# Down-projection loads of `final_g` and of the residual on other queues; the output projection's weights split during the attention, kept in DRAM, and read back as halves by GpSimd

## The chip, the cores and the metric

The kernel runs on one core of one Trainium2 chip. The metric is the device time of one execution in microseconds; of the kernel before there are three runs. A core has TensorE (PE in the rows, matrix products), VectorE (DVE), ScalarE (ACT), GpSimd (POOL) and SyncE (SP, which here only issues transfers). Each engine works through its own list in order; engines wait for one another by semaphores. Transfers between DRAM and the on-chip memory are issued by an engine (an instruction that ends once the transfer is handed over) and carried by 16 DMA engines that all queues share.

## What is computed

One inference step of a one-layer decoder: 1024 prompt rows and 8 x 4 = 32 sample rows, 1024 features, in float32.

```python
mod = jax.nn.silu(c) @ w_ada + b_ada            # shift, scale, gate, twice
h = _rmsnorm(x, norm1_g) * (1 + sc1) + sh1
mix, new_conv, new_kv = _mixer(h, w_in, conv_w, gn_conv, gn_attn, w_out, rel_bias, conv_prev, kv_bufs)
x = x + ga1 * mix                               # output projection: mixed @ w_out
h2 = _rmsnorm(x, norm2_g) * (1 + sc2) + sh2
ffn = (jax.nn.silu(h2 @ w_gate) * (h2 @ w_up)) @ w_down
x = x + ga2 * ffn
y = _rmsnorm(x, final_g)
```

The mixer is one input projection `w_in` into convolution inputs and queries, keys and values; a short convolution; dilated window attention in three groups of four heads (rows of the prompt among themselves, sample rows against caches); a norm; and the output projection `w_out` (1024 x 1024). The caches, moved on by four rows, are outputs too.

## The kernel before

**Numbers.** Every float32 product is made as three products of rounded halves: high x high, low x high, high x low. So each weight tile is loaded (`load_raw`, L117: a tile of 128 x 1024, 512 KB, in one of three slots of the tag `raw`), its high half `wh` is made by ScalarE (`split_high`, through the helper at L93) and its low half `wl` = raw - wh by VectorE (`split_raw`, L136). The tags `wh` and `wl` have two slots each; a slot is free once the last reader of the tile in it is done. Activations have halves as well (`mh`/`ml`, `xh`/`xl`, `ah`/`al`).

**Stages,** in order of time: to 67 us the first norm and the conditioning; 67 to 484 us the input projection, tile by tile of 128 columns (`proj_res`, three products of column blocks of 384, 384 and 288 rows each), woven with the prompt attention of six pairs (group g, pair j) and the sample attention. In the loop over g and j, a pair's three tiles (key, query, value) are multiplied, then `prompt_pair` runs; products of the pair after are woven into it. 484 to about 608 us is the output projection: `w_out_tile(m)` (L1182) loads and splits tile m with SP, ScalarE and VectorE; tiles 0 to 7 are multiplied with column blocks 0 and 1 of the mixer's output, and once more, loaded and split again, with blocks 2 and 3 (16 tiles in all). Meanwhile `mixed` (L1106 on) makes the halves `mh` and `ml` of the next block, `squares` and `norm2_square` add up sums of squares, and the second norm (`modulate`, L265 to L276) and `combos(0)` (L1215 on: sums of column blocks and their halves `xh`, `xl`, for a fast matrix product with seven multiplications) prepare the FFN. 608 to 1081 us is gate and up of the FFN; GpSimd makes the sums of weights that the fast product needs (L1325 to L1328) and stores each finished block of silu(gate) x up to `a_d` in DRAM (L1420). From 1105 us the down projection runs in four chunks: `load_a` (L1468) loads the six pieces `a` of a chunk from `a_d`, on SP, into slots of the tag `raw`, and ScalarE and VectorE make `ah` and `al`; `load_down` loads `w_down` tiles into the same three slots; the residual `x2m` is read from `xT_d` (8 pieces of 528 KB).

**What sets the order.** Each engine's list is in the order in which the scheduler of the language places the instructions; `high_priority` moves a load or a split ahead as far as its slots allow, `in_order` and `issue_after` place one behind another. Engine and queue are written in the code: `nc.gpsimd.tensor_sub` is GpSimd's arithmetic, `nc.sync.dma_start` a transfer issued by SP. The copies of the caches (L1412) are issued by SP, two after each FFN step, the remaining ones behind the last weights. In `mixed`, GpSimd makes three of four `ml` (`k % 4`); in `squares` and `norm2_square` the argument `eng` names the engine that adds.

## Time and profile before

| | us |
|---|---|
| median of 3 runs | 1382.58 (1374.85 to 1383.36) |
| profiled execution, its own time | 1384.71 |
| its span in the profile | 1382.9 |
| TensorE busy | 1304.9 (94%) |
| VectorE busy | 722.4 (52%) |
| ScalarE busy | 505.1 (37%) |
| GpSimd busy | 252.5 (18%) |
| bytes moved | 199.81 MB, mean 144 GB/s |

The page and the views of the trace count an engine as busy while an instruction of it runs (issuing a transfer, waiting and semaphores are not counted). A row's "idle before" is the time in which the engine stood still just before that instruction, and the name behind the arrow is what ended it. The granted clock (PEclk) is TensorE's clock as a share of its upper level of 2.4 GHz; the lower level is 1.2 GHz, or 0.50. Times in the rows are in us from the span's start; L12 is line 12 of the kernel before.

### The profile page before, as it was taken

Reading aid. Unit: us, or ns where it says so; the run is one execution under the profiler, and the core shown is the slowest. Engines: PE = TensorE matmul, PEld = TensorE weight load, DVE = VectorE, ACT = ScalarE, POOL = GpSimd, SP = SyncE. Lnnn points to the kernel's source line nnn. Section 1 sums busy time; section 2 is a strip of 40 time slices with the busy share of each in tenths; the row PEclk is TensorE's granted clock in tenths of the full one; section 3 lists DMA queues with packets and bytes.
Section 4 is the critical chain, followed back from the end, with each engine's and each line's share of the span. In section 5 each row is a group of like instructions: output and inputs, shape, how many; then the busy total and the mean of one; then the engine's idle time right before and its main releaser. Section 6 shows DMA issues by size and latency. Waiting matters only on the chain.

```text
span 1382.9 us, 23582 instructions
## 1 busy us (share of the span) xinstructions
PE 1304.9 (94%) x9488; PEld 1207.1 (87%) x9488; DVE 722.4 (52%) x1399; ACT 505.1 (37%) x1085; POOL 252.5 (18%) x251
## 2 busy tenths in 40 slices
PE   8999999998999989897999999999999399999996
PEld 7777686887779879887999999999999299999996
DVE  5722364155227767889654466455445335353466
ACT  5432414243342255646334334333334202020244
POOL 3700000000000146354222334223212100000000
PEclk9999999998989999999999999999999799999998
DMA  9975371247336624464352634333250824141344
GB/s 313 302 243 166 103 264 48 67 126 225 99 102 173 178 71 154 139 218 136 110 192 84 227 93 168 123 108 110 90 205 32 307 58 140 46 140 47 94 145 133
DMA packets 189500, 199.81 MB, mean 144 GB/s; under 512 B 11786, under 2 KB 166919, under 8 KB 188880
## 3 DMA queue, kind: packets, MB, share of 16 engines
q1 hardware_dynamic: 176718, 173.76, 39.7%
q0 software_dynamic: 5600, 20.59, 4.1%
q10 hardware_dynamic: 7074, 3.97, 1.1%
q8 instruction: 74, 1.21, 0.4%
q14 instruction: 34, 0.28, 0.1%
HBM read 169.53 MB, written 55.82 MB: 163 GB/s over the span
## 4 chain that ended last, share of the span: by engine, by line
PE 76%; DVE 8%; DMA 8%; ACT 3%; issue 3%; POOL 1%; SPq 1%; DVEq 0%; ACTq 0%; POOLq 0%
PE pss L1381 6%; PE pss L1382 6%; PE pss L1383 6%; PE psmm L161 5%; PE psmm L162 4%; PE psmm L163 4%; PE pss L1494 3%; PE pss L1495 3%; PE pss L1496 3%; PE psmm L1494 3%; PE psmm L1495 3%; PE psmm L1496 3%; DMA qb<-qs_d 3%; PE pss L683 3%; PE psmm L1381 3%; PE psmm L1382 3%
## 5 line engine op out<-in xcount | busy, mean ns | idle before, releaser
L93 ACT ACTIVATE wh<-raw 128x512 fp32r<-128x512 f32 (+2 forms) x208 | 160.9, 785 | 423.1 <-PE psmm L162 96.7
L1381 PE MATMUL pss<-xh,wh 128*128 128x264 f32 x704 | 201.3, 286 | 5.2 <-DVE sg L1358 2.3
L1383 PE MATMUL pss<-xh,wl 128*128 128x264 f32 x704 | 201.2, 286 | 2.6 <-DVE wl L1318 2.5
L1382 PE MATMUL pss<-xl,wh 128*128 128x264 f32 x704 | 201.1, 286 | 1.8 <-DVE xl L1227 1.8
L161 PE MATMUL psmm<-hh,wh 128*128 128x384 f32 (+1 forms) x528 | 176.8, 335 | 2.3 <-DVE ring L1041 1.4
L162 PE MATMUL psmm<-hl,wh 128*128 128x384 f32 (+1 forms) x528 | 175.3, 332 | 0.0
L163 PE MATMUL psmm<-hh,wl 128*128 128x384 f32 (+1 forms) x528 | 174.9, 331 | 0.0
L136 DVE TENSOR_TENSOR wl<-raw,wh 128x1024 fp32r<-128x1024 f32 (+2 forms) x111 | 117.1, 1056 | 78.2 <-ACT wh L93 77.2
L1318 DVE TENSOR_TENSOR wl<-raw,wh 128x512 fp32r<-128x512 f32 x96 | 90.1, 950 | 115.6 <-ACT wh L93 112.5
L1381 PEld LDWEIGHTS pss<-xh,wh 128*128 128x128 f32 x704 | 133.5, 190 | 6.5 <-DVE sg L1358 2.5
L1383 PEld LDWEIGHTS pss<-xh,wl 128*128 128x128 f32 x704 | 132.7, 189 | 3.7 <-DVE wl L1318 3.6
L1382 PEld LDWEIGHTS pss<-xl,wh 128*128 128x128 f32 x704 | 133.4, 189 | 2.1 <-DVE xl L1227 2.1
L161 PEld LDWEIGHTS psmm<-hh,wh 128*128 128x128 f32 x528 | 101.0, 191 | 16.5 <-issue 12.9
L1494 PE MATMUL pss<-ah,wh 128*128 128x384 f32 (+1 forms) x264 | 86.5, 328 | 23.8 <-ACT wh L93 23.8
L163 PEld LDWEIGHTS psmm<-hh,wl 128*128 128x128 f32 x528 | 101.4, 192 | 3.1 <-issue 2.7
L162 PEld LDWEIGHTS psmm<-hl,wh 128*128 128x128 f32 x528 | 100.9, 191 | 3.2 <-issue 2.9
L1381 PE MATMUL psmm<-xh,wh 128*128 128x264 f32 x352 | 101.0, 287 | 1.4 <-ACT p L93 0.8
L1383 PE MATMUL psmm<-xh,wl 128*128 128x264 f32 x352 | 100.8, 286 | 0.4 <-DVE wl L1318 0.4
L1382 PE MATMUL psmm<-xl,wh 128*128 128x264 f32 x352 | 100.9, 287 | 0.0
L1495 PE MATMUL pss<-al,wh 128*128 128x384 f32 (+1 forms) x264 | 86.3, 327 | 0.0
L1496 PE MATMUL pss<-ah,wl 128*128 128x384 f32 (+1 forms) x264 | 86.1, 326 | 0.0
L1495 PE MATMUL psmm<-al,wh 128*128 128x384 f32 (+1 forms) x264 | 85.5, 324 | 0.0
(327 smaller groups left out, 2925.6 us busy)
## 6 DMA issues: line engine op xcount, KB each, us to landing
ring<-in_w_ada_dram SPq DMA_DIRECT2D x32, 512.0 KB
out_dram<-in_cache_kv_dram SPq DMA_DIRECT2D x8, 2040.0 KB
raw<-in_w_in_dram SPq DMA_DIRECT2D x24, 512.0 KB
raw<-in_w_gate_dram SPq DMA_DIRECT2D x24, 512.0 KB
raw<-in_w_up_dram SPq DMA_DIRECT2D x24, 512.0 KB
a_d<-sg POOLq DMA_DIRECT2D x22, 528.0 KB, 3.7
a<-a_d SPq DMA_DIRECT2D x22, 528.0 KB
raw<-in_w_down_dram SPq DMA_DIRECT2D x48, 192.0 KB
```

Source lines behind the costliest of these rows:

```text
L93: return nc.scalar.activation(out, in_, func, **kw)
L136: nc.vector.tensor_sub(wl[:, :nk], raw[:, :nk], wh[:, :nk].bitcast(F32))
L161: nc.tensor.matmul(out, wh[:, k], h, start=(i == 0), stop=False)
L162: nc.tensor.matmul(out, wh[:, k], l, start=False, stop=False)
L163: last = nc.tensor.matmul(out, wl[:, k], h, start=False, stop=(i == n - 1))
L1318: nc.vector.tensor_sub(wl[:, 4 * i:4 * i + 4], x, h.bitcast(F32))
L1381: nc.tensor.matmul(o, wh[:, k0 + k], hi[:, k], start=st, stop=False, skip_group_check=True)
L1382: nc.tensor.matmul(o, wh[:, k0 + k], lo[:, k], start=False, stop=False, skip_group_check=True)
L1383: last = nc.tensor.matmul(o, wl[:, k0 + k], hi[:, k], start=False, stop=(k == 3), skip_group_check=True)
L1494: nc.tensor.matmul(o[:, :n], wh, ah[:, t0:t0 + n], start=(j == 0), stop=False)
L1495: nc.tensor.matmul(o[:, :n], wh, al[:, t0:t0 + n], start=False, stop=False)
L1496: nc.tensor.matmul(o[:, :n], wl, ah[:, t0:t0 + n], start=False, stop=(j == 2 * nf - 1))
```

## The change

1. `fg` (`final_g` to 128 rows) was loaded by ScalarE's queue at the start of the last chunk; now GpSimd's queue loads it after `load_a(0)`. The eight residual pieces `x2m` were loaded by GpSimd's queue; now SP loads each behind the weights of its tile in the first chunk.
2. `split_out(m)` loads tile m of `w_out`, splits it and has GpSimd store both halves in DRAM (`wo_d[m]`): one tile after each pair of the attention, two in group 1. `w_out_tile` no longer loads and splits: GpSimd issues two loads of 512 KB, the high half into a slot of `raw`, the low half in turn into a slot of `wh` or `wl`.
3. The additions that GpSimd did around the output projection (`ml`, sums of squares, `combos(0)`, the sample columns in `modulate`) are VectorE's.

```diff
--- before.py
+++ after.py
@@ -105,6 +105,7 @@
     strip_d = dr.tile([12, NSTRIP], F32, name="strip_d")
     st_d = dr.tile([3, 64, P], F32, name="st_d")
     wgt_d = dr.tile([3, 32, P], F32, name="wgt_d")
+    wo_d = [dr.tile([2, P, D], F32R, name=f"wo_d{m}") for m in range(KT)]
     qs_d = dr.tile([3, NS, 256], F32, name="qs_d")
 
     def rstd_from(ss_ap, n, out_ap):
@@ -272,8 +273,8 @@
         if n_p < n:
             tv = x[:, :, o + n_p:o + n]
             t4 = tv.rearrange("p k (b t) -> p k b t", t=NT)
-            nc.gpsimd.tensor_mul(t4, t4, bcast(amod[:, 1, :, 1:9], 3, NT))
-            nc.gpsimd.tensor_add(t4, t4, bcast(modt[:, 3, :, 1:9], 3, NT))
+            nc.vector.tensor_mul(t4, t4, bcast(amod[:, 1, :, 1:9], 3, NT))
+            nc.vector.tensor_add(t4, t4, bcast(modt[:, 3, :, 1:9], 3, NT))
 
     w_in_v = w_in[0].rearrange("(k p) c -> p k c", p=P)
 
@@ -911,6 +912,14 @@
             else:
                 nc.vector.tensor_scalar(bss[g][:, P:], mask[:, 1], new[:, 0:1], None, op0=ALU.add)
 
+    w_out_v = w_out[0].rearrange("(k p) c -> p k c", p=P)
+
+    def split_out(m):
+
+        for i, x in enumerate(split_raw(load_raw(w_out_v[:, :, P * m:P * m + P], KT), KT)):
+            nc.gpsimd.dma_start(wo_d[m][i].rearrange("p (k c) -> p k c", c=P), x)
+
+    out_split = iter(range(KT))
     bss = [cp.tile([P, 160], F32, name=f"bs{g}") for g in range(3)]
 
     yt = []
@@ -947,6 +956,8 @@
             store_kvp(g, k_n, 0, j, 7 if g == 0 else (1 if g == 1 else 0))
             if j and g == 0:
                 sample_bias()
+            for _ in range(2 if g == 1 else 1):
+                split_out(next(out_split))
         stats_out(g)
         queues["any"].append(sample_scores(g, *sample_new(g, qs, ks, vs)))
         yt += qs
@@ -1093,7 +1104,7 @@
     feats = [(c, 0) for c in conv] + [(y, DIL[i // 2]) for i, y in enumerate(yt)]
     acc_y = squares(feats[2:], 0, nc.vector)
     rb_y = rstd_rows(acc_y, 0, 768, "rbb1", after_gate, "pt")
-    acc_m = squares(feats[2:], 1, nc.gpsimd)
+    acc_m = squares(feats[2:], 1, nc.vector)
     conv_gate(1)
 
     m_hi = [[unit(ua, "mh", (P, 2, NSUB), F32R) for _ in range(4)] for _ in range(2)]
@@ -1115,12 +1126,10 @@
                 nc.vector.scalar_tensor_tensor(dst(t[:, sl]), src(x), sv[:, gcol:gcol + 1], dst(rbb[:, sl]),
                                                op0=ALU.mult, op1=ALU.mult)
             act(hi, t[:, :n])
-            eng = nc.gpsimd if k % 4 else nc.vector
-            eng.tensor_sub(m_cols(m_lo, tb, k), t[:, :n], hi.bitcast(F32))
-
-    w_out_v = w_out[0].rearrange("(k p) c -> p k c", p=P)
+            nc.vector.tensor_sub(m_cols(m_lo, tb, k), t[:, :n], hi.bitcast(F32))
+
     order = list(range(2, KT)) + [0, 1]
-    rot = [0]
+    rot = [0, 0]
 
     def psb():
         rot[0] += 1
@@ -1180,7 +1189,13 @@
         return last
 
     def w_out_tile(m):
-        return load_w(w_out_v[:, :, P * m:P * m + P], KT)
+        hi = wp.tile([P, T], F32R, tag="raw", bufs=3, name=nm("wh"))[:, :D].rearrange("p (k c) -> p k c", c=P)
+        rot[1] += 1
+        lo = wp.tile([P, KT, P], F32R, tag=("wh", "wl")[rot[1] % 2], bufs=2, name=nm("wl"))
+        with tc.high_priority():
+            for i, x in enumerate((hi, lo)):
+                nc.gpsimd.dma_start(x, wo_d[m][i].rearrange("p (k c) -> p k c", c=P))
+        return hi, lo
 
     acc_x = {}
 
@@ -1209,7 +1224,7 @@
         mixed(tb, range(2), rstd_rows(acc[1], tb, 256, "rbb0", after))
 
     def mixed_squares(tb):
-        return squares(feats[2:], tb, nc.gpsimd), squares(feats[:2], tb, nc.gpsimd)
+        return squares(feats[2:], tb, nc.vector), squares(feats[:2], tb, nc.vector)
 
 
 
@@ -1256,9 +1271,9 @@
     for m in range(2, KT):
         w_o = w_out_tile(m)
         out_product(w_o, m, 0)
-        norm2_square(0, m, nc.gpsimd)
+        norm2_square(0, m, nc.vector)
         last = out_product(w_o, m, 1)
-        norm2_square(1, m, nc.gpsimd if m < 6 else nc.vector)
+        norm2_square(1, m, nc.vector)
         if m == 3:
             sample_merge()
             acc_m = mixed_squares(3)
@@ -1278,7 +1293,7 @@
         norm2_square(2, m, nc.vector)
         out_product(w_o, m, 3)
         norm2_square(3, m, nc.vector)
-    combos(0, [ua] * 4 + [ub] * 3, nc.gpsimd)
+    combos(0, [ua] * 4 + [ub] * 3, nc.vector)
     xa.release()
     w3 = tc.alloc_tile_pool(name="w3", bufs=1, reuse_waits="tile")
     w1 = tc.alloc_tile_pool(name="w1", bufs=1, reuse_waits="tile")
@@ -1497,22 +1512,22 @@
         add_gated(5, m, t0, n, x2m[m][:, t0:t0 + n], o)
 
     a = load_a(0)
-    for m in range(KT):
-        x = (d1 if m < 7 else d2).tile([P, T], F32, tag="x2", bufs=7 if m < 7 else 1, name=nm("x2"))
-        nc.gpsimd.dma_start(x, xT_d[:, m])
-        x2m.append(x)
+    fg = d2.tile([P, D], F32, name="fg")
+    nc.gpsimd.dma_start(fg, bcast(final_g, 0, P))
     for c, (f0, nf) in enumerate(CHUNKS):
         if f0 + nf < FH:
             for m in range(KT):
                 w = load_down(f0, nf, m)
+                if c == 0:
+                    x = (d1 if m < 7 else d2).tile([P, T], F32, tag="x2", bufs=7 if m < 7 else 1, name=nm("x2"))
+                    nc.sync.dma_start(x, xT_d[:, m])
+                    x2m.append(x)
                 for t0, n in TBS:
                     down(w, a, nf, m, t0, n)
             a = load_a(c + 1)
             continue
         with in_order(silu[0]):
             nc.scalar.preload_act_table_set("natural_log_exp_and_others")
-        fg = d2.tile([P, D], F32, name="fg")
-        nc.scalar.dma_start(fg, bcast(final_g, 0, P))
         for tb, (t0, n) in enumerate(TBS):
             for m in range(KT):
                 down(load_down(f0, nf, m), a, nf, m, t0, n)
```

How this moves the lists, at three places. First, ScalarE in the attention, at what the trace of before has from 183 to 210 us (`ring` are the emptied products of `w_in` tiles, `wh` the high halves). Before:

```order
L93 ACTIVATE wh_1529<-raw_1527 128x1024
L93 ACTIVATE ring_1396<-psmm_1403 128x384
L93 ACTIVATE ring_1396<-psmm_1448 128x384
L93 ACTIVATE wh_1904<-raw_1902 128x1024
L93 ACTIVATE ring_1396<-psmm_1487 128x256
L93 ACTIVATE ring_1396<-psmm_1487 128x32
L93 ACTIVATE ring_1526<-psmm_1533 128x384
L93 ACTIVATE ring_1526<-psmm_1571 128x384
L93 ACTIVATE wh_2042<-raw_2040 128x1024
```

Now:

```order
L93 ACTIVATE wh_1545<-raw_1543 128x1024
L93 ACTIVATE ring_1412<-psmm_1419 128x384
L93 ACTIVATE ring_1412<-psmm_1464 128x384
L93 ACTIVATE wh_1885<-raw_1883 128x1024
L93 ACTIVATE ring_1412<-psmm_1503 128x256
L93 ACTIVATE ring_1412<-psmm_1503 128x32
L93 ACTIVATE wh_1928<-raw_1926 128x1024
L93 ACTIVATE ring_1542<-psmm_1549 128x384
L93 ACTIVATE ring_1542<-psmm_1587 128x384
L93 ACTIVATE wh_2066<-raw_2064 128x1024
```

One `wh` more (`wh_1885`, from the first `w_out` tile of that stretch) stands between the emptied products, and the next `w_in` tile's `wh_1928` comes later in the list.

Second, SP where the down projection begins (`a` are the pieces of the FFN's result, `x_16..` to `x_17..` the residual, `raw` the `w_down` tiles, `out_dram` the last cache copies). Before:

```order
L1412 DMA out_dram<-in_cache_kv_dram 16x16256 x2
L1412 DMA out_dram<-in_cache_kv_dram 16x3968 x8
L1472 DMA a_11554<-a_d_83 128x1056
L1472 DMA a_11560<-a_d_83 128x1056
L1472 DMA a_11566<-a_d_83 128x1056
L1472 DMA a_11572<-a_d_83 128x1056
L1472 DMA a_11578<-a_d_83 128x1056
L1472 DMA a_11584<-a_d_83 128x1056
L1487 DMA raw_11606<-in_w_down_dram 128x3x128 x2
L1487 DMA raw_11676<-in_w_down_dram 128x3x128 x2
L1487 DMA raw_11746<-in_w_down_dram 128x3x128 x2
```

Now:

```order
L1427 DMA out_dram<-in_cache_kv_dram 16x3968 x8
L1487 DMA a_11594<-a_d_83 128x1056
L1487 DMA a_11600<-a_d_83 128x1056
L1487 DMA a_11606<-a_d_83 128x1056
L1523 DMA x_1687_11639<-xT_d 128x1056
L1487 DMA a_11612<-a_d_83 128x1056
L1487 DMA a_11618<-a_d_83 128x1056
L1487 DMA a_11624<-a_d_83 128x1056
L1523 DMA x_1695_11711<-xT_d 128x1056
L1502 DMA raw_11632<-in_w_down_dram 128x3x128 x2
L1502 DMA raw_11704<-in_w_down_dram 128x3x128 x2
L1523 DMA x_1703_11783<-xT_d 128x1056
```

The residual pieces, which stood in GpSimd's list, are now between the `a` pieces and the `w_down` tiles.

Third, GpSimd in the output projection (`acx` sums of squares, `ml` low halves; `wo_d` the stored halves of `w_out`). Before:

```order
L1197 TENSOR_TENSOR acx_5003<-acx_5003,sq_5424 128x272
L1197 TENSOR_TENSOR acx_5129<-acx_5129,sq_5453 128x256
L1197 TENSOR_TENSOR acx_5003<-acx_5003,sq_5488 128x272
L1197 TENSOR_TENSOR acx_5129<-acx_5129,sq_5517 128x256
L1119 TENSOR_TENSOR ml_4914<-mx_5525,mh_4906 128x256
L1119 TENSOR_TENSOR ml_4914<-mx_5530,mh_4906 128x256
L1119 TENSOR_TENSOR ml_4915<-mx_5540,mh_4907 128x256
L1119 TENSOR_TENSOR ml_4916<-mx_5545,mh_4908 128x256
```

Now, at about the same place:

```order
L1197 DMA wh_5456<-wo_d_94 128x1024
L1197 DMA wl_5519<-wo_d_95 128x1024
L1197 DMA wl_5457<-wo_d_94 128x1024
L1197 DMA wh_5518<-wo_d_95 128x1024
L1197 DMA wl_5629<-wo_d_96 128x1024
L1197 DMA wh_5628<-wo_d_96 128x1024
L1197 DMA wl_5691<-wo_d_97 128x1024
L1197 DMA wh_5690<-wo_d_97 128x1024
```

GpSimd's list there holds loads and no additions; the additions stand in VectorE's list.

## Rows read from the trace of the kernel before

**Rows 1.** The page, busy time of two engines: us, share of the span, instructions

```profile
PE 1304.9 (94%) x9488; PEld 1207.1 (87%) x9488; DVE 722.4 (52%) x1399; ACT 505.1 (37%) x1085; POOL 252.5 (18%) x251
```

**Rows 2.** Table of stretches: engines' busy us (instructions), clock, DMA share, GB/s

```profile
core 0: us, PE busy (x) PEld busy (x) DVE busy (x) ACT busy (x) POOL busy (x), PEclk, DMA share, GB/s
300.00:320.00 20.00, 20.00 (x129) 20.00 (x128) 15.08 (x24) 4.42 (x6) 0.00 (x0) 1.00 0.89 278
320.00:340.00 20.00, 15.78 (x85) 13.06 (x83) 11.79 (x28) 6.73 (x17) 1.05 (x2) 0.80 0.74 224
480.00:680.00 200.00, 179.29 (x1320) 168.43 (x1320) 155.41 (x235) 111.31 (x223) 89.81 (x77) 0.96 0.45 140
580.00:600.00 20.00, 15.28 (x110) 14.62 (x108) 20.00 (x23) 8.98 (x12) 9.10 (x3) 0.91 0.19 55
1090.00:1100.00 10.00, 0.00 (x0) 0.00 (x0) 3.77 (x3) 3.25 (x3) 2.17 (x5) 0.50 1.03 411
```

**Rows 3.** Waits: engine, line, waited for; us in total, times, longest

```profile
PE pss L1494 <- ACT wh L93: 23.8, 1, 23.8
```

**Rows 4.** Waits of SP's queue from 1040 to 1130 us

```profile
SPq L1412 <- DMA fg<-in_final_g_dram: 51.4, 1, 51.4
```

**Rows 5.** Timeline of SP: start us, us, line, operation, count

```profile
1012.91 63.92 SPq L1412 DMA_DIRECT2D out_dram<-in_cache_kv_dram  x10
1077.00 10.64 SPq L1472 DMA_DIRECT2D a<-a_d  x6
```

**Rows 6.** Timeline of ScalarE before the down projection

```profile
1081.11 1.08 ACT L93 ACTIVATE ah<-a 128x1056 fp32r<-128x1056 f32 x1 [7.80 <-DMA a<-a_d]
...
1091.15 1.08 ACT L93 ACTIVATE ah<-a 128x1056 fp32r<-128x1056 f32 x1 [5.14 <-DMA a<-a_d]
...
1104.21 0.84 ACT L93 ACTIVATE wh<-raw 128x768 fp32r<-128x768 f32 x1 [7.72 <-DMA raw<-in_w_down_dram]
```

**Rows 7.** Timeline of VectorE at the same place

```profile
1081.30 0.43 DVE L1355 TENSOR_TENSOR sg<-sg,pss 128x264 f32<-128x264 f32 x1 [1.05 <-PE pss L1383]
1082.22 1.26 DVE L1477 TENSOR_TENSOR al<-a,ah 128x1056 fp32r<-128x1056 f32 x1 [0.49 <-ACT ah L93]
```

**Rows 8.** The tile `a_d`: its stores' ns (min/median/max), and their landing

```profile
L1420 POOL DMA_DIRECT2D a_d<-sg x22: 670/682/827, 652.1 to 1082.0; - x22
...
DMA to landing us min/median/max: 3.1/3.7/9.4
```

**Rows 9.** DMA issues from 1076 to 1104 us: count, KB each, median us to landing

```profile
x<-xT_d POOLq DMA_DIRECT2D x8, 528.0 KB, 9.1
```

**Rows 10.** Groups by line, 480 to 680 us: busy us, mean ns; idle before, releasers

```profile
L163 PE MATMUL pss<-mh,wl 128*128 128x272 f32 (+1 forms) x128 | 39.0, 305 | 4.7 <-DVE wl L136 4.7
...
L136 DVE TENSOR_TENSOR wl<-raw,wh 128x1024 fp32r<-128x1024 f32 x19 | 24.0, 1261 | 6.0 <-ACT wh L93 6.0
...
L1381 PE MATMUL pss<-xh,wh 128*128 128x264 f32 x80 | 23.8, 298 | 4.7 <-DVE sg L1358 2.3 <-ACT xh L93 1.9 <-ACT p L93 0.4
L1382 PE MATMUL pss<-xl,wh 128*128 128x264 f32 x80 | 23.6, 295 | 1.8 <-DVE xl L1227 1.8
...
L1227 DVE TENSOR_TENSOR xl<-x,xh 128x1056 fp32r<-128x1056 f32 x14 | 22.4, 1618 | 0.4 <-ACT xh L93 0.4
...
L1119 DVE TENSOR_TENSOR ml<-mx,mh 128x272 fp32r<-128x272 f32 (+1 forms) x8 | 5.7, 716 | 0.0
```

**Rows 11.** The same stretch by form of operation, VectorE

```profile
L1236 DVE TENSOR_TENSOR x<-x 128x1056 f32<-128x1056 f32 x1 | 2.3, 2341 | 0.0
```

**Rows 12.** Groups by form, 680 to 1080 us, VectorE

```profile
L1355 DVE TENSOR_TENSOR sg<-sg,u 128x264 f32<-128x264 f32 x21 | 9.2, 439 | 0.7
```

**Rows 13.** Waits in 480 to 680 us

```profile
POOL x L1234 <- DVE xl L1227: 17.9, 1, 17.9
```

**Rows 14.** Timeline of ScalarE in the attention

```profile
183.63 1.06 ACT L93 ACTIVATE wh<-raw 128x1024 fp32r<-128x1024 f32 x1 [12.99 <-PE psmm L162]
...
197.42 1.06 ACT L93 ACTIVATE wh<-raw 128x1024 fp32r<-128x1024 f32 x1 [2.95 <-PE psmm L162]
```

## The prediction

> **What bounds the kernel now.** I read the page's busy table first [rows 1]: TensorE works in 94% of the span, VectorE in half of it. So only two things can give time: TensorE's idle time (1382.9 - 1304.9 = 78 us) and stretches in which its granted clock is at the lower level. The table of stretches [rows 2] then says where the two lie. From 300 to 320 us TensorE is never idle, though the DMA engines are 0.89 busy. From 320 to 340 it has a stall, after which the mean granted clock is 0.80. In 480 to 680 us (output projection, second norm, start of the FFN) it is idle for 200.0 - 179.3 = 20.7 us; in 580 to 600, where it loses 4.7 us of these, VectorE is busy without a break (20.00 of 20). From 1090 to 1100 it does nothing at all, while the DMA engines are full (1.03, 411 GB/s). That last hole is the passage from the FFN's gate/up to the down projection; the waits of TensorE [rows 3] make it the longest of all: one wait of 23.8 us, for the high half of the first w_down tile. Elsewhere TensorE runs without gaps, and nothing that the change does there can be gained.
>
> **Part 1: the passage to the down projection (x2 and final_g).** Why is that first half late? Backward through the rows: ScalarE makes it at 1104.21, having waited 7.72 us for the w_down load [rows 6]. That load needs one of three `raw` slots, which the six `a` pieces hold; the first `a` piece comes only at 1081.11, after 7.80 us of waiting [rows 6]. SP issues the `a` loads only from 1077.00 on [rows 5], because the last cache copies ahead of them in its order stood for 51.4 us behind one wait: for the load of final_g [rows 4], which ScalarE issues at the very end of the FFN. Once loose, the six `a` loads, the 8 x2 loads of 528 KB on GpSimd's queue (9.1 us to land, [rows 9]) and the weights share the full DMA engines, so that the fourth `a` (needed to free a slot) is split at 1091.15.
> The change takes final_g out of that chain (GpSimd loads it after its last a_d store), and SP's order puts x2 piece 0 behind three `a`, x2 piece 1 before the first w_down tile, the others behind later weights (order, second place). Now SP reaches the `a` loads in time, and three of them lie in their slots before the last gate/up product. Their high halves can be made at about 1074, but VectorE's low halves stand behind the FFN's last product at 1081.30 + 0.43 [rows 7]: the three follow at 1.26 us each, 1083.0, 1084.3, 1085.5. The fourth `a` is issued at 1083, lands 3.7 us later (the median of a_d stores of the same size, [rows 8]), at 1086.7; with 1.08 + 1.26 it frees its slot at 1089. Then 393 KB of w_down: some 2.5 us by its size against 528 KB in 3.7, and 0.84 of ScalarE: TensorE starts at about 1092.5. The bytes give a second bound: two a_d stores, x2 pieces 0 and 1, three `a`, final_g and w_down 0 are seven times 0.54 plus 0.52 plus 0.39 = 4.7 MB, which at 0.38 MB/us (the level of [rows 2] in this hole, a little under 411) is 12.4 us from 1081.3: 1093.7 + 0.84 = 1094.5. Before, it started at 1104.21 + 0.84 = 1105.1. I take 1094: **-11 us**, between -4 (x2 piece 1 waits for the last a_d store, whose longest landing is 9.4, [rows 8], and w_down stands behind it on SP) and -15 (TensorE at 1090).
>
> **Part 2: the output projection.** 16 weight splits leave this stage: 16 passes of ScalarE, which has room, and 16 x 1.261 = 20.2 us of VectorE [rows 10]. GpSimd issues 32 loads of 512 KB in their place (order, third place); the nearest row are the a_d stores, of that size and on that queue: 0.68 to issue and 3.7 to land, 9.4 at most [rows 8]. A tile's 48 products (8 row blocks, 3 products, 2 column blocks) take TensorE 48 x 179.29/1320 = 6.5 us [rows 2], so 2 x 0.68 of issue and 1 MB per tile fit. The loads run three tiles ahead for high halves, four for low ones. GpSimd's arithmetic moves to VectorE: 24 low halves `ml`, 17 + 10 sums of squares, 4 sums in `combos(0)` and 2 products of the sample rows. Their price on VectorE: with GpSimd at work beside it, `ml` took 0.716 [rows 10] and a sum of 1056 columns 2.34 [rows 11]; without, an add of 264 columns took 0.439 and the al subtraction of 1056 columns 1.26 [rows 7, 11, 12]. So between 53 x 0.44 + 4 x 1.26 = 28 us and 53 x 0.72 + 4 x 2.34 = 48 us. Since GpSimd's arithmetic is gone from most of the stage, I take 30. VectorE is at 155.4 of 200 us now [rows 2]; 155.4 - 20.2 + 30 = 165, and what is left also gets cheaper: the 14 `xl` of 1618 ns [rows 10] would take 1.26 as `al` does, -5 us. So VectorE is no fuller than before, and its work is not in the same places: the `wl` on which TensorE waited 4.7 us [rows 10] are gone, and the 4.7 + 1.8 us that the FFN's first products waited for `sg`, `xh` and `xl` [rows 10] came with a `combos(0)` that ran late: GpSimd's first sum waited 17.9 us for an `xl` [rows 13]. On VectorE it stands right behind that `xl`, during the second pass of the output projection. The trap of a new wait: the `ml`, one per product of the next column block, now stand in VectorE's order beside the residual adds. I take half of the 20.7 us: **-10 us**, between 0 and -18 (nearly all of the idle time, with a few us of slow clock behind the stalls).
> *A rule and the rows.* A sum of 1056 columns takes VectorE 2.34 us beside GpSimd's, a subtraction of that size 1.26 with GpSimd idle [rows 7, 11]; I priced most of the moved work at the lower level, since GpSimd is then idle. The Trainium skill, SBUF — State Buffer, section Who interferes with whom, gives the reason: a VectorE instruction with two SBUF inputs contends with a GpSimd instruction that reads SBUF, and the later one waits. By it the moved work costs 28 us and VectorE comes to 163 of 200; by the dear rows 48 and 183, which is the first rival. The same page's section 🔬 SBUF: two separate sides speaks against the change: a load that GpSimd issues waits for its descriptors while VectorE runs a two-port form, and it gives 3.1 us for 0.62; estimated from that page, two loads would take 6.2 us of GpSimd's time per tile, under the tile's own, so the sum would stay.
>
> **Part 3: the attention pays.** The 8 splits of w_out move into 67 to 484 us: one after each pair, two in the middle group. Each adds a 512 KB read, a ScalarE and a VectorE pass (1.06 and 1.26), and two stores of 512 KB that GpSimd issues. ScalarE and VectorE have room there, so the passes cost nothing themselves; they hide under a w_in tile's products, 13.8 us of TensorE (the `wh` of two tiles start at 183.63 and 197.42, [rows 14]). The catch is the slots: `wh` and `wl` have two each, and one turn of them is now a split's. The order of ScalarE (first place below) shows `wh_1928` behind `wh_1885`; it can be written only when the stores out of that slot have landed. Chain: 1.06 + 1.26 + 0.68 + 3.7, then 1.06 + 1.26 for the next tile = 9.0 us: it fits 13.8. With the longest landing (9.4) it is 14.7, or 0.9 too long. With two splits in a row (2 pairs) it is 6.7 + 6.7 + 2.3 = 15.7, some 2 us too long each, 27 at the longest landing, 13 too long. Added to it is the clock: the stall of some 4 us in 320 to 340 left it at half for a while, and its slice fell to 0.80 [rows 2], 4 us of work lost. So two stalls of 2 us: **+4 us**, between -2 (ring loads earlier, since the bias loads have moved up in SP's order) and +44 (both longest cases everywhere: 4 x 0.9 + 2 x 13 = 30, and clock losses of 14).
>
> **Sum.** 1384.7 (profiled execution) - 11 - 10 + 4 = 1367.7. That execution stands 2.1 us over the median of 1382.58, so the median comes to **1366 us**.
>
> **Rivals.**
> - *VectorE fills up* in 484 to 620: it is the one engine at 20.00 of 20 [rows 2], and the `ml` of one column block, `combos(0)` and the residual adds queue on it. For it: 28 to 48 us added against 20 removed. Against it: the 5 us of relief from `xl`. Then part 2 gives -2: 1382.58 - 11 - 2 + 4 = 1374.
> - *x2 ahead of the weights:* the wait of x2 piece 1 for the last store holds the first w_down on SP; only -5 of part 1: 1372.
> - *The other side: the stores' round trip.* On DMA engines at 0.89 [rows 2] each split's stores land late, and `wh` of the next w_in tile keeps ScalarE, and behind it the emptying of PSUM, waiting. Price +44: 1382.58 - 21 + 44 = 1406. It decides above 35/8, about 4.4 us a split, for slower by 1%; above 2.6 a split for no gain.
> - *Both* of the first two, with splits at 2 us each (+16): 1382.58 - 5 - 2 + 16 = 1392.
> - *The change does not do what it says:* the copies still stand behind something on SP: final_g's wait is gone from the order, so the chance is small, within the second rival.
>
> **How the numbers follow.** About 1% is what a measurement of this kernel can tell from no change: 1368.8 and 1396.4 are the bounds. Forecast 0.5 (own range 1356 to 1374, of it 0.4 under 1368.8); VectorE full 0.17; x2 ahead 0.13; round trip 0.1; both 0.1. Faster: 0.4 + 0.05 + 0.05 = 0.50. Slower: 0.1 + 0.02 = 0.12. Same: 0.38. The range leaves out the round trip (0.1) and the worse half of both (0.05) above 1392, and 0.05 below 1353 (the best ends of all parts together give 1382.58 - 15 - 18 - 2 = 1348).
>
> **What would show it.** Right: in the new trace the idle time before the first w_down product is 13 us, not 23.8, SP shows no wait for final_g, and the `a` loads start before 1070; in the output projection no wait of TensorE for a low half, and GpSimd only issuing; the slices of 300 to 320 and around stay full. Wrong: waits of `wh` in the attention for GpSimd's stores with TensorE idle behind them (part 3), waits for w_out halves (part 2), or SP standing at x2 while weights are due (part 1).

## The result and the profile after

Over 20 executions of each, the changed kernel takes 1374.4 us in the median (1361.87 to 1380.72) and the kernel before 1379.74 us (1374.85 to 1384.06, and one execution of 1827.24 that the ratio leaves out); the ratio is 0.9948, with a 95% interval of 0.9928 to 0.9967. That is half a per cent faster: the right side, inside the range of 1353 to 1392, but a gain of 5 us by the medians and 7 by the ratio where 17 were forecast, and less than the 1% named as the bound for "faster". The profiled execution has a span of 1375.2 us (1382.9 before; that one, of 1384.71 us, is slower than any of the other 19 of its kernel).

The rows that answer to those of before. The table of stretches, as [rows 2]:

```profile
300.00:320.00 20.00, 20.00 (x117) 15.54 (x117) 7.87 (x24) 3.65 (x10) 0.00 (x0) 0.78 0.27 86
320.00:340.00 20.00, 20.00 (x124) 20.00 (x123) 16.44 (x26) 6.09 (x8) 1.07 (x2) 1.00 0.95 300
480.00:680.00 200.00, 181.30 (x1356) 171.32 (x1355) 149.82 (x290) 97.61 (x209) 47.96 (x54) 0.97 0.60 196
580.00:600.00 20.00, 20.00 (x166) 20.00 (x165) 17.29 (x35) 8.62 (x14) 3.12 (x6) 1.00 0.62 183
1090.00:1100.00 10.00, 2.65 (x8) 2.48 (x9) 5.69 (x5) 4.16 (x5) 0.00 (x0) 0.50 1.01 333
```

In 580 to 600 us TensorE no longer stalls and VectorE has room (17.29 of 20). In 300 to 320, full and fast before, the clock is now 0.78. The waits of the whole run, as [rows 3]:

```profile
DVE wl L137 <- DMA wo_d<-wl: 42.9, 8, 8.7
PE pss L1509 <- ACT wh L93: 14.7, 1, 14.7
PE pss L1396 <- ACT wh L93: 9.6, 1, 9.6
```

The first is a wait that did not exist: VectorE stands 42.9 us in eight places until a stored half has left its slot. The second is the old hole of 23.8 us, now 14.7. The third is new as well, in the first FFN step. The groups of 480 to 680 us, as [rows 10]:

```profile
L164 PE MATMUL pss<-mh,wl 128*128 128x272 f32 (+1 forms) x128 | 37.4, 292 | 0.3 <-DMA wl<-wo_d 0.3
...
L1396 PE MATMUL pss<-xh,wh 128*128 128x264 f32 x77 | 23.0, 299 | 12.8 <-ACT wh L93 9.6 <-ACT p L93 2.3 <-DVE sg L1373 1.0
...
L1242 DVE TENSOR_TENSOR xl<-x,xh 128x1056 fp32r<-128x1056 f32 x14 | 19.7, 1410 | 0.3 <-ACT xh L93 0.3
...
L1129 DVE TENSOR_TENSOR ml<-mx,mh 128x272 fp32r<-128x272 f32 (+1 forms) x32 | 12.6, 429 | 0.9 <-ACT mh L93 0.9
```

The 4.7 us for `wl` are 0.3; an `ml` takes VectorE 429 ns, not 716.

For all kernels below, one table. Its times are read from the trace: the start of the first product that reads `mh` (the output projection), from there to the first that reads `xh` (its length), from the first to the last that reads `xh` and a weight's high half (FFN), and TensorE's wait before the first w_down product. The first column lies some 10 us behind the 484 of the list of stages, since TensorE still has products of the input projection after 484. Each row is one profiled execution; the ratio is over several.

| kernel | output proj. starts | its length | FFN | wait w_down | ratio to before (95%) |
|---|---|---|---|---|---|
| before | 493.8 | 117.7 | 469.2 | 23.8 | 1 |
| after | 506.8 | 102.0 | 473.4 | 14.7 | 0.9948 (0.9928 to 0.9967) |
| again (after, second profile) | 493.1 | 101.9 | 471.3 | 15.1 | |
| passage | 488.3 | 117.8 | 468.4 | 14.6 | 0.9926 (0.9899 to 0.9954) |
| fg_only | 487.2 | 117.8 | 468.3 | 22.4 | 0.9989 (0.9971 to 1.0008) |
| splits_unread | 504.7 | 117.8 | 469.9 | 24.8 | 1.0087 (1.0057 to 1.0117) |
| splits_unstored | 486.0 | 117.7 | 469.9 | 23.1 | 0.9995 (0.9974 to 1.0016) |
| six_splits | 499.2 | 104.1 | 472.8 | 15.2 | 0.9901 (0.9877 to 0.9924) |
| second_pass | 490.7 | 111.6 | 471.5 | 14.4 | 0.9905 (0.9884 to 0.9927) |
| arith_dve | 492.3 | 108.0 | 489.9 | 22.9 | 1.0082 (1.0059 to 1.0105) |
| arith_pool | 500.3 | 116.6 | 478.0 | 14.4 | 1.0116 (1.0083 to 1.0149) |
| ffn_order | 512.5 | 101.9 | 466.9 | 14.9 | 0.9925 (0.9894 to 0.9956) |
| reread_order | 487.5 | 112.9 | 465.6 | 14.3 | 0.9847 (0.9821 to 0.9872) |
| six_order | 493.5 | 104.3 | 465.2 | 15.3 | 0.9835 (0.9810 to 0.9859) |

The second row read against the first is the whole account of that execution: +13.0 before the output projection, -15.7 in it, +4.2 in the FFN, -9.1 in the passage, together -7.6 of the 7.7 us by which the spans differ.

### The profile page after: what moved, and what is told of

It reads as the page before. It is cut to its first block, busy times and chain, and to the rows that moved or that the text cites. A ratio compares the mean times of both kernels' runs of the same rounds, so it can differ in the third digit from the quotient of the medians.

```text
span 1375.2 us, 23628 instructions
## 1 busy us (share of the span) xinstructions
PE 1307.9 (95%) x9488; PEld 1206.0 (88%) x9488; DVE 716.9 (52%) x1448; ACT 499.6 (36%) x1077; POOL 212.1 (15%) x235
## 4 chain that ended last, share of the span: by engine, by line
PE 73%; DVE 9%; issue 8%; DMA 7%; POOL 2%; ACT 1%; SPq 1%; DVEq 0%; POOLq 0%; ACTq 0%
PE pss L1398 6%; PE pss L1397 6%; PE pss L1396 6%; PE psmm L162 4%; PE psmm L163 4%; PE psmm L164 4%; PE pss L1509 3%; PE pss L1510 3%; PE pss L1511 3%; PE psmm L1509 3%; PE psmm L1510 3%; PE psmm L1511 3%; PE psmm L1397 3%; PE psmm L1396 3%; PE psmm L1398 3%
## 5 line engine op out<-in xcount | busy, mean ns | idle before, releaser
L93 ACT ACTIVATE wh<-raw 128x512 fp32r<-128x512 f32 (+2 forms) x200 | 152.7, 775 | 440.4 <-PE psmm L163 91.2
L137 DVE TENSOR_TENSOR wl<-raw,wh 128x1024 fp32r<-128x1024 f32 (+2 forms) x103 | 107.3, 1043 | 97.8 <-ACT wh L93 54.1
L1396 PEld LDWEIGHTS pss<-xh,wh 128*128 128x128 f32 x704 | 133.4, 190 | 13.7 <-ACT wh L93 9.8
L162 PEld LDWEIGHTS psmm<-hh,wh 128*128 128x128 f32 x528 | 100.8, 191 | 14.7 <-issue 11.5
L1397 PE MATMUL psmm<-xl,wh 128*128 128x264 f32 x352 | 100.6, 286 | 0.0
L1509 PE MATMUL pss<-ah,wh 128*128 128x384 f32 (+1 forms) x264 | 86.2, 326 | 14.7 <-ACT wh L93 14.7
L1509 PE MATMUL psmm<-ah,wh 128*128 128x384 f32 (+1 forms) x264 | 85.4, 324 | 0.0
```

What stands on the lines that cost most here:

```text
L93: return nc.scalar.activation(out, in_, func, **kw)
L137: nc.vector.tensor_sub(wl[:, :nk], raw[:, :nk], wh[:, :nk].bitcast(F32))
L162: nc.tensor.matmul(out, wh[:, k], h, start=(i == 0), stop=False)
L1396: nc.tensor.matmul(o, wh[:, k0 + k], hi[:, k], start=st, stop=False, skip_group_check=True)
L1397: nc.tensor.matmul(o, wh[:, k0 + k], lo[:, k], start=False, stop=False, skip_group_check=True)
L1509: nc.tensor.matmul(o[:, :n], wh, ah[:, t0:t0 + n], start=(j == 0), stop=False)
```

## The experiments

**The passage: which of the two moves?** `passage` is part 1 of the diff on the kernel before; `fg_only` moves final_g alone:

```diff
-        nc.scalar.dma_start(fg, bcast(final_g, 0, P))     # in the last chunk
+    nc.gpsimd.dma_start(fg, bcast(final_g, 0, P))         # behind the x2 loads, which stay with GpSimd
```

> The kernel before with part 1 alone (final_g by GpSimd after its last store, residual pieces by SP behind the weights of their tile). In the changed kernel's trace TensorE stands 14.7 us before the first w_down product, 23.8 before the change. Theory: the passage is a sum of its own, so the wait falls to 14 to 15.5 us here too and the time by 8 to 10 us, ratio 0.993 to 0.994, which is more than the whole change gave. Rival: part of it comes from GpSimd and VectorE being emptier late in the FFN of the changed kernel; then the wait stays above 18 us and the ratio is 0.997 or more.

> The kernel before, in which final_g alone moves (to GpSimd, behind the residual loads there); the residual pieces stay with GpSimd. Theory that the wait for final_g held SP: SP reaches the a loads before 1070 us, three a pieces are in early, the wait before the first w_down product falls from 23.8 to 15 to 19 us, ratio 0.994 to 0.998; what is missing to passage (0.9926) is the residual pieces' share of the full DMA engines. Rival, the residual loads are the bound: the wait stays above 21 us, ratio 0.998 to 1.002.

`passage` alone is worth 0.9926, the wait is 14.6 us: at least as much as the whole change (the two intervals overlap). `fg_only` is worth nothing that can be measured, and here the rival was right. SP is free early, and the high halves of three `a` are made from 1065.75 on, yet the rest is nearly as late as ever. ScalarE's timeline in `fg_only`:

```profile
1065.75 3.02 ACT L93 ACTIVATE ah<-a 128x1056 fp32r<-128x1056 f32 x3
1080.06 1.08 ACT L93 ACTIVATE ah<-a 128x1056 fp32r<-128x1056 f32 x1 [11.29 <-DMA a<-a_d]
...
1095.31 0.84 ACT L93 ACTIVATE wh<-raw 128x768 fp32r<-128x768 f32 x1 [8.49 <-DMA raw<-in_w_down_dram]
```

After the last `a`, ScalarE waits 8.49 us for the first weights, a load of 393 KB (7.72 before, [rows 6]). The eight residual pieces (4.3 MB, landing in a median of 9.1 us as in [rows 9]) were issued by GpSimd from 1075 to 1083, the weights by SP from 1082 on. In the changed kernel only three of them are issued before that load has landed; SP's timeline there:

```profile
1029.69 41.00 SPq L1487 DMA_DIRECT2D a<-a_d  x3
1075.26 0.32 SPq L1523 DMA_DIRECT2D x<-xT_d  x1
1084.34 2.66 SPq L1487 DMA_DIRECT2D a<-a_d  x3
1087.71 0.32 SPq L1523 DMA_DIRECT2D x<-xT_d  x1
1091.62 2.18 SPq L1502 DMA_DIRECT2D raw<-in_w_down_dram  x4
```

And ScalarE's:

```profile
1074.68 3.02 ACT L93 ACTIVATE ah<-a 128x1056 fp32r<-128x1056 f32 x3
1089.22 1.08 ACT L93 ACTIVATE ah<-a 128x1056 fp32r<-128x1056 f32 x1 [11.51 <-DMA a<-a_d]
...
1096.45 0.84 ACT L93 ACTIVATE wh<-raw 128x768 fp32r<-128x768 f32 x1 [1.70 <-DMA raw<-in_w_down_dram]
```

The wait for the weights is 1.70. What moves is TensorE's last FFN product to its first w_down product, 24.4 us before and 15.2 after. So final_g's place alone does nothing, and what is left of the edit is the residual's. Whether the residual alone would do it, without final_g, was not run.

**The attention: what do the splits cost there, and by what?** `splits_unread` adds the eight splits and stores to the kernel before, with nothing that reads them; `splits_unstored` leaves out the stores (the diff shows it against `splits_unread`); `again` is the changed kernel without any edit:

```diff
-        for i, x in enumerate(split_raw(load_raw(w_out_v[:, :, P * m:P * m + P], KT), KT)):
-            nc.gpsimd.dma_start(wo_d[m][i].rearrange("p (k c) -> p k c", c=P), x)
+        split_raw(load_raw(w_out_v[:, :, P * m:P * m + P], KT), KT)
```

> The kernel before, with the eight extra splits of w_out and their stores in the attention, and nothing reading them (the output projection splits its weights again). Slot theory (VectorE's low half of the next w_in tile waits for the stores out of its slot, the sample attention and the softmax stand behind it, and the clock falls): the first product of the output projection moves from 493.8 us to 503 to 508, the ratio is 1.007 to 1.011. Traffic theory (the added 12.6 MB hold up the qb loads): the same. Chance theory (the clock of the attention falls by itself from execution to execution): no move beyond 3 us in the median, ratio 0.998 to 1.002.

> The same, but the halves are not stored: eight reads of 512 KB and eight splits stay, the stores go and with them the wait of a slot for a store. Slot theory: what is left is the work of the splits, which has room: the output projection starts at 493 to 497 us, ratio 0.999 to 1.003. Traffic theory: a third of the bytes, a third of the cost, start at 497 to 500, ratio 1.002 to 1.004. Chance theory: ratio 0.998 to 1.002.

> The changed kernel once more, for a second profile: which of its stalls and slow stretches come back. Slot theory: the stalls near 214, 283 and 351 us and VectorE's waits for wo_d stores (42.9 us in all) come back, the stretch at half clock from 285 to 309 us too. Chance theory: stalls come back, the long slow stretch not or elsewhere, and the output projection starts 5 us or more from 506.8. The 9.5 us wait in the first FFN step, behind ScalarE, comes back by every theory.

With stores 1.0087 and a start at 504.7; without, 0.9995 and 486.0. The reads, the splits and their place in the lists cost nothing that can be measured, the stores everything. The waits of `splits_unread` name the slot:

```profile
DVE wl L137 <- DMA wo_d<-wl: 41.6, 8, 8.9
```

The low half's store is issued second, and lands late. The issues of the changed kernel (count, KB each, median us to landing; the high halves' stores have 4.3):

```profile
wo_d<-wl POOLq DMA_DIRECT2D x8, 512.0 KB, 6.8
```

What stands behind such a wait shows in VectorE's timeline of the changed kernel:

```profile
209.55 1.23 DVE L137 TENSOR_TENSOR wl<-raw,wh 128x1024 fp32r<-128x1024 f32 x1 [1.72 <-DMA wo_d<-wl]
...
213.56 0.41 DVE L220 COPY adasb<-pso 128x256 f32<-128x256 f32 x1
...
279.33 1.22 DVE L137 TENSOR_TENSOR wl<-raw,wh 128x1024 fp32r<-128x1024 f32 x1 [5.65 <-DMA wo_d<-wl]
...
280.81 1.22 DVE L137 TENSOR_TENSOR wl<-raw,wh 128x1024 fp32r<-128x1024 f32 x1
...
282.44 0.28 DVE L691 CUSTOM_DVE_ANT_0 p<-pss,bias 128x128 f32<-128x128 f32 x1
```

And in TensorE's, the first score product that has to wait for that softmax step:

```profile
282.78 0.70 PE L684 MATMUL pss<-ring,ring 64*128 64x256 f32 x3 [1.59 <-DVE stt L691]
```

Two low halves, the first held 5.65 us by a store, come ahead of the first softmax step, and TensorE stands 1.59 us. That is little. But the clock falls after it. The table of stretches, 284 to 309 us, of the changed kernel (columns as [rows 2]):

```profile
284.00:309.00 25.00, 25.00 (x102) 14.42 (x101) 6.53 (x32) 10.36 (x37) 0.00 (x0) 0.52 0.24 72
```

The same stretch in `splits_unread`:

```profile
284.00:309.00 25.00, 25.00 (x99) 14.50 (x98) 6.70 (x34) 10.32 (x38) 0.00 (x0) 0.52 0.25 74
```

And in `again`:

```profile
284.00:309.00 25.00, 25.00 (x176) 19.21 (x175) 12.74 (x48) 10.28 (x35) 0.00 (x0) 1.00 0.42 130
```

At 0.52, the 1.2 GHz level, 102 products get done where the other level does 176; by these counts about 10.5 of the 25 us are lost. `again` is the same program with the same stalls (3.9, 1.6 and 5.4 us of TensorE near 214, 282 and 339; 4.5, 1.6 and 6.0 in the first profile), and it keeps the upper level from 284 to 309: its output projection starts at 493.1 instead of 506.8. The table of stretches from 67 us to that start, the changed kernel first, then `again`:

```profile
67.00:506.80 439.80, 426.07 (x2792) 340.60 (x2791) 195.17 (x527) 145.89 (x371) 14.31 (x28) 0.94 0.57 176
67.00:493.10 426.10, 412.81 (x2789) 333.55 (x2788) 194.65 (x527) 145.25 (x371) 14.27 (x28) 0.98 0.59 181
```

TensorE is idle for 13.7 and 13.3 us; the whole difference is busy time at a lower clock, 10.5 us of it behind the stall near 282 and some 3 from 425 to 434 us, where the changed kernel's profile has a mean of 0.64 and `again` no fall. (The kernel before falls as well, from 405 to 418.)

Of the five profiles with eight stored splits three fell to 0.50 to 0.52 in this stretch (`ffn_order` is the third), `arith_pool` had 0.93 and `again` 1.00; the nine others, none of which has the stall near 282 us, all had 1.00. So slot theory and chance theory each hold a part: the store makes the stall, and whether the stall costs 1.6 us or, with the fall of the clock behind it, some 12 differs from execution to execution. That the stall sets off the fall is read from this count (three of five with it, none of nine without); no run has the stall by other means. The changed kernel's 20 executions fit that: the fastest has a mean granted clock of 0.982, the slowest 0.963, and 19 us between them (9 in the kernel before), more than one such fall.

The other two stalls are not new. TensorE in the kernel before:

```profile
211.23 0.44 PE L222 MATMUL pspt<-ident,adasb 128*128 128x128 f32 x2 [2.43 <-DVE adasb L219]
332.98 1.00 PE L683 MATMUL pss<-ring,ring 64*128 64x128 f32 x4 [4.22 <-DVE stt L690]
```

In the two profiles of the changed kernel they are longer by 1 to 2 us each.

The theory of traffic was not tried apart from the slot (the same bytes from elsewhere), nor a slot of its own for the splits. But the sign of that theory, longer waits for the `qb` loads, did not come. VectorE's waits for them in the kernel before and in `splits_unread`:

```profile
DVE qb L803 <- DMA qb<-qs_d: 20.2, 11, 3.5
DVE qb L804 <- DMA qb<-qs_d: 17.4, 13, 3.8
```

`six_splits` makes one split after each pair, and treats tiles 0 and 1 where they are first used:

```diff
-            for _ in range(2 if g == 1 else 1):
-                split_out(next(out_split))
+            split_out(next(out_split))                  # tiles 2 to 7
-    w_o = [w_out_tile(m) for m in range(2)]
+    w_o = [w_out_first(m) for m in range(2)]            # load_w, then both halves stored by GpSimd
```

> The changed kernel with one split after each pair only (tiles 2 to 7); tiles 0 and 1 are loaded and split where the output projection first uses them, and stored then. Double theory: it is the second split of a pair that puts a second low half ahead of the first softmax on VectorE (the 1.6 us stall near 282 us, behind which the clock may fall for 24 us); it goes, no slow stretch between 285 and 309 in any run, the spread of the runs falls under 12 us (19 before), the median comes to 1362 to 1368, ratio 0.987 to 0.992. Rival, the single splits stall as well (near 214 and 340 us, 4 and 5 us): ratio 0.992 to 0.996.

As the theory of the second split says: no stall near 282, clock 1.00 there, 0.9901, and 8.6 us between the six executions. (The clock is that of one profile; `six_order`, below, has 1.00 there as well. There are also two splits fewer in the attention, so the second split of a pair is not the only thing that went.) The single splits go on stalling: 5.7 us at 216 and 7.2 at 341.

**The output projection: splits or additions?** `second_pass` has no split in the attention, and takes `w_out_first` for all eight tiles of the first pass:

```diff
-            for _ in range(2 if g == 1 else 1):
-                split_out(next(out_split))
+    def w_out_first(m):
+        w = load_w(w_out_v[:, :, P * m:P * m + P], KT)
+        for i, x in enumerate(w):
+            nc.gpsimd.dma_start(wo_d[m][i].rearrange("p (k c) -> p k c", c=P), x)
+        return w
```

`arith_dve` is point 3 of the change alone, on the kernel before, and `arith_pool` the changed kernel with point 3 undone; of `arith_dve`, two of its eight places:

```diff
-            eng = nc.gpsimd if k % 4 else nc.vector
-            eng.tensor_sub(m_cols(m_lo, tb, k), t[:, :n], hi.bitcast(F32))
+            nc.vector.tensor_sub(m_cols(m_lo, tb, k), t[:, :n], hi.bitcast(F32))
-    combos(0, [ua] * 4 + [ub] * 3, nc.gpsimd)
+    combos(0, [ua] * 4 + [ub] * 3, nc.vector)
```

> The changed kernel without splits in the attention: the first pass of the output projection loads and splits its weights as before the change and stores the halves, the second pass reads them. Slot theory: the attention is as before the change (output projection from 486 to 490 us), the second pass has no stall for a low half; the first pass has its eight splits and the added sums on VectorE. Output projection 102 to 110 us long, ratio 0.985 to 0.990. Rival, VectorE is too full in the first pass with splits and sums together: 114 us or more, ratio 0.992 to 0.996.

> The kernel before with part 3 alone: the additions of GpSimd around the output projection are VectorE's, the weights are split twice as before. Theory that the splits were the load: VectorE has both, the output projection gets longer than its 117 us (120 to 125), the start of the FFN is no better, ratio 1.001 to 1.007. Rival, the additions on GpSimd were what stalled TensorE and slowed VectorE: 108 to 113 us, ratio 0.992 to 0.997.

> The changed kernel with part 3 undone: GpSimd adds again around the output projection, the halves still come from DRAM by GpSimd's loads. arith_dve showed 107.7 us of output projection for 117.3 and a FFN 20 us longer; this is the other side. Theory that both the additions and the splits held the output projection: 105 to 112 us for 101.6, the loads wait behind GpSimd's additions, FFN 468 to 472, ratio 0.996 to 1.001. Rival, the splits alone did: 101 to 103 us, ratio 0.991 to 0.995.

The lengths of the output projection: 117.7 with splits and additions as before, 108.0 with the additions moved, 111.6 with the additions moved and the first pass splitting and storing, 116.6 with the splits gone but the additions on GpSimd, 102.0 with both moved. I had the splits as the burden, and it is the additions first: `arith_dve` came out on its rival's side in this stage. `second_pass`, with 111.6 and 0.9905, lies between what its theory and its rival gave. Yet alone each of the two moves makes the kernel slower: both `arith_dve` (1.0082) and `arith_pool` (116.6 us and 1.0116) lie outside everything that was expected of them. `arith_dve` pays 20.7 us in the FFN (TensorE's waits for weight halves and `xl` from 604 to 664 us, and one of 3.75 us at 849; what makes those halves late there was not followed); `arith_pool` keeps the attention's cost, and pays 8.8 in the FFN. Why the loads alone save nothing was not followed to its end; in its list GpSimd's loads and additions alternate, and 11.3 us of TensorE's waiting stand in its first FFN step (9.6 in the changed kernel).

**The FFN's start: an order that nobody asked for.** ScalarE's timeline of the changed kernel there:

```profile
626.98 1.07 ACT L93 ACTIVATE xh<-x 128x1056 fp32r<-128x1056 f32 x1
627.96 2.42 ACT L93 ACTIVATE x<-x,modt,amod 128x224 f32<-128x224 f32 x5
630.96 1.08 ACT L93 ACTIVATE xh<-x 128x1056 fp32r<-128x1056 f32 x1 [0.59 <-DVE x L1249]
632.32 1.09 ACT L93 ACTIVATE xh<-x 128x1056 fp32r<-128x1056 f32 x1 [0.28 <-DVE x L1253]
633.32 1.04 ACT L93 ACTIVATE wh<-raw 128x1024 fp32r<-128x1024 f32 x1
```

The weight half `wh` of the up block, for which TensorE waits 9.55 us until 634.41, comes from a load that was issued at 602.97. But the scheduler placed it behind four `xh` of the second half of the columns (the first at 625.54), two of which wait for VectorE's sums. In the kernel before it came ahead of them (625.66, the first of those `xh` at 630.91). `ffn_order` asks for that again (the `xh` of `combos(1)` behind the weight half), `reread_order` and `six_order` ask more, on top of `second_pass` and `six_splits`:

```diff
+        if second is not None:
+            with in_order(last_split[0]):               # last_split: the ACT split of the newest weight block
+                second()                                # the norm of the last column block
-            act(hi, src)
+            with in_order(last_split[0] if s else None):
+                act(hi, src)
```

> The changed kernel with one wish for the order: the halves xh of the second half of the columns come on ScalarE behind the first weight half of the first up block (as it was in the kernel before). Order theory: the 9.6 us wait of TensorE in the first FFN step is ScalarE's list, in which four xh, each waiting for VectorE's sums, stand ahead of that weight half; the wait falls under 2 us, the FFN's length from 471 to 473 to 462 to 466 us, the ratio is 0.987 to 0.990. Rival, VectorE is the bound there (19.9 of 20 us busy from 620 to 640): other waits take its place, the FFN stays at 469 or more, ratio 0.993 to 0.996.

> second_pass (no splits in the attention, first pass splits and stores, second pass reads) with a stronger wish for the order: the norm of the last column block and the xh halves come behind the first weight half of the first up block. Order theory: the 9.6 us wait of the first FFN step, 4.6 with the weaker wish, falls under 2 us, the FFN is 460 to 465 us long for 471.5, ratio 0.983 to 0.988 (second_pass 0.9905). Rival, VectorE is the bound there and the waits move to xl and sums behind it: FFN 468 or more, ratio 0.989 to 0.991.

> six_splits with the same stronger wish. Order theory: FFN 460 to 465 us for 472.8, ratio 0.982 to 0.987 (six_splits 0.9901). The single splits in the attention still stall near 216 and 341 us, so no better than reread_order by more than 3 us. Rival: FFN 468 or more, ratio 0.989 to 0.991.

The weak wish brings 9.55 to 4.55 us, and the FFN from 471 to 473 down to 466.9; its total is unclear against the changed kernel (0.9925 and 0.9948, with intervals that overlap; its profile fell to the lower clock for all of 284 to 309). With the strong wish the FFN is 465.6 and 465.2 us long, 6 to 8 less than in the kernels that they build on. The totals gain 0.6%. In `reread_order` the half comes ahead of the `xh`:

```profile
615.38 0.37 ACT L93 ACTIVATE sg<-pss 128x264 f32<-128x264 f32 x1
615.65 1.05 ACT L93 ACTIVATE wh<-raw 128x1024 fp32r<-128x1024 f32 x1
616.60 0.62 ACT L93 ACTIVATE wh<-sw 128x512 fp32r<-128x512 f32 x1
617.12 1.07 ACT L93 ACTIVATE xh<-x 128x1056 fp32r<-128x1056 f32 x1
```

The wait is down to 1.8 us in both, though the FFN stays just above the 460 to 465 us expected. VectorE, the rival, is not the bound at this place. Both versions beat both kernels: 1357.5 us for `six_order` (0.9835) and 1360.5 for `reread_order` (0.9847), with the kernel before at 1378.1 beside them; between the two nothing is settled.

## Why the prediction was right and wrong

- **What bounds the kernel:** right. TensorE's idle time and its clock carried every difference.
- **Part 1, -11:** the size held (-9.2 from the last gate/up product to the first w_down product; `passage` 0.9926, about -10). The working gave SP's wait for final_g as the head of the chain and the residual's loads as one of three that share the engines; `fg_only` shows that the first alone is worth nothing measurable. The step that failed is reading the longest wait of a queue as the cause: with it gone, the next one (the residual's 4.3 MB ahead of 0.4 MB of weights) holds the same place. By the steps, each landing took longer than I took it (the fourth `a` 4.9 us for 3.7, the weights 4.8 for 2.5), and the fourth `a` was issued a little later; the second bound, by bytes, had 1094.5, and TensorE began at 1097.3 of an FFN that ended 1.4 later.
- **Part 2, -10:** the sum held, its parts did not. The output projection itself gave 15.7, more than the 10 taken; about half of it is TensorE's idle time (9.0 us before, 1.4 after), the rest busy time (108.7 and 100.6 us, at a mean clock of 0.96 and 1.00), which the working had left to its upper bound. The start of the FFN, where part of the gain was to come from, lost 2 to 4: the 6.5 us of waits that I counted as gone with a late `combos(0)` were replaced by the 9.6 us behind ScalarE's order. The working goes through VectorE's and GpSimd's work at this place and not through ScalarE's list.
- **A rule and the rows:** the low price was right; `ml` 429 ns and not 716 once GpSimd no longer adds, as the Trainium skill, SBUF — State Buffer, section Who interferes with whom, has it. The two other kernels agree: 428 in `arith_dve`, 566 in `arith_pool`, where GpSimd adds again. The relief of `xl` came in part, 1410 ns for the 1260 taken. VectorE comes to 149.8 of 200 us, under the 163 worked out from the low price (the stage starts 13 us later, so the 200 us do not hold quite the same work). The starved descriptors did not show: GpSimd issues a load of `wo_d` in 0.54 us each time, with VectorE 17.29 of 20 us busy. No row tells whether VectorE ran a two-port form then, so that rule is not tested by it.
- **Part 3, +4:** the mis-sized term, and the cause of the missing gain. The mechanism was there (two slots, one turn more, a store's landing before the next half), at VectorE's low half rather than ScalarE's high one. That the double splits would stall most holds for TensorE's new stall near 282 only: VectorE's longest waits (7.6, 8.7 and 7.9 us near 82, 146 and 405) lie behind single splits, the four of the double ones are of 1.7 to 6.0. Five profiles with stored splits start the output projection at 503.5 us on average (493.1 to 512.5), seven without at 489.4: +14. The three with the long fall of the clock start at 508.0 on average, the two without it at 496.7. The +4 was two stalls at their own length; a loss by the clock stands in the working, but only the upper bound of +44 carries one (14). In this stretch of small products 1.6 us of stall was followed by a loss of some 10 in three profiles of five.
- **The rivals:** the round trip of the stores came true in mechanism at a third of its price (1.8 us a split), under the 2.6 from which it takes all the gain. VectorE did not fill up in the output projection (it is busy for 19.86 of 20 us from 620 to 640, but there ScalarE's order was the bound); x2 did not block SP (its wait for the last store is 0.6 us). "The copies still stand behind something" did not come. The median of 1374.4 is the first rival's number without the first rival's mechanism, and just above the forecast's own 1356 to 1374. That it lies well inside 1353 to 1392 is in part luck: the output projection gave more than was taken, and the attention took that and more.
- **The sum** with the measured parts: -9 -15.7 +4 +14 = -7, beside 5 by the medians and 7 by the ratio (single profiles and means over several are mixed in it, so it is not good to a microsecond). The 10 us that were missing went back in the attention.

## What to carry to other kernels

Work that is moved out of a full stage into one "with room" takes slots along, and where each engine keeps its list in order, the price is paid by what stands behind the first waiting instruction: count the round trip of a store against the time until the slot's next writer, and prefer one such trip at a time. After every move, read the list of each engine at the seams, those too that the change does not name; a scheduler may put a ready and needed piece behind four that wait, and one wish for the order was worth as much as the change. And the longest wait of a queue is not yet the cause of what is late: ask what would hold the same place next.

## What the runs showed of the hardware

- A stall of 1.6 us in a stretch of small products was followed by 24 to 27 us at the lower clock level in three of five profiles, and by hardly any in two, one of them of the same program. The Trainium skill, TensorE: Matmul & The Clock Gate, section A second HAM failure mode: psum-queue depth-cycling, tells of frequent small idle times between groups of products, by which the clock goes up and down between its two levels. The rows here have the two levels (0.52 and 1.00 in the same stretch), but behind a single stall, and TensorE is busy for all of the 25 us that follow; whether it is the same thing, no run shows. That the fall comes in some executions only fits the 19 us over which the changed kernel's times spread, and no run here shows what decides it.
- Stores and loads of 512 KB on GpSimd's queue took 3.2, 5.4 and 9.8 us to land (least, median, most) in the changed kernel; the median is half as much again as the 3.7 of [rows 8], from which I had estimated it, and that of the low halves' stores alone 6.8.
